# A loop of 62 rounds over four 50 KB buffers in place of straight code, in a log-softmax

## Chip, cores and metric

The kernel runs on one core of a Trainium2 chip. The metric is device time in microseconds (us), median over the executions of a kernel; lower is better. All executions quoted here were fast (granted TensorE clock 1.00). A ratio is the mean time of one kernel's fast runs over that of the kernel before in the same rounds on the same chip, with a 95% interval; it is not quite the ratio of the medians that stand beside it.

## The reference

`x` is float32 of shape (16, 512, 50000): 8192 rows, 1638.4 MB in and as much out.

```python
max_x = np.max(x, axis=-1, keepdims=True)
shifted = x - max_x
log_sum_exp = np.log(np.sum(np.exp(shifted), axis=-1, keepdims=True))
return (shifted - log_sum_exp).astype(np.float32)
```

## The kernel before

A row lies on G = 8 partitions, so that a tile is 16 rows: 128 partitions of 6250 columns (25,000 bytes), 512 tiles. There are 8 buffers. SyncE issues the loads, ScalarE's queue issues the stores, and each store writes from the buffer that its load filled. The program is straight code: the Python loop emits every tile with constant addresses.

```python
G = 8; R = P // G; EXP_C = 3125; NBUF = 8; AHEAD = 7
    xt = xf.rearrange("(t r) (g w) -> t (r g) w", r=R, g=G)
    ot = of.rearrange("(t r) (g w) -> t (r g) w", r=R, g=G)
    data = ctx.enter_context(tc.tile_pool(name="data", bufs=NBUF))
# ... (other pools, the matrix of ones)
    def load(t):
        buf = data.tile([P, W], FP32, name="buf")
        nc.sync.dma_start(out=buf, in_=xt[t])
        tiles[t] = buf
    def front(t):
        buf = tiles[t]
        pmax = stats.tile([P, 1], FP32, name="pmax")
        nc.vector.reduce_max(out=pmax, in_=buf, axis=AX)
        # ... two transposes, a reduction and a copy: negmax, the row's own maximum
        for j in range(nexp):                                   # 2 pieces
            nc.scalar.activation(
                out=dump, in_=buf[:, j * EXP_C : (j + 1) * EXP_C], func=ACT.Exp,
                bias=negmax[:, 0:1], scale=1.0, accum_out=part[:, j : j + 1],
            )
        # ... 2 matmuls with ones: rowsum;  Ln: logsum
    def back(t):
        buf = tiles.pop(t)
        nc.vector.tensor_scalar(
            out=buf, in0=buf, scalar1=shift.pop(t)[:, 0:1], scalar2=logs.pop(t),
            op0=ALU.add, op1=ALU.subtract,
        )
        nc.scalar.dma_start(out=ot[t], in_=buf)

    for t in range(AHEAD):
        load(t)
    for t in range(ntiles + 1):
        if t < ntiles: front(t)
        if t >= 1: back(t - 1)
        if t + AHEAD < ntiles: load(t + AHEAD)
```

Of the kernel before, what the change touches and what calls it, by code (L numbers as in the profile page):

```python
# [1 line left out]

# [4 lines left out]


FP32 = mybir.dt.float32
ACT = mybir.ActivationFunctionType  # L10
ALU = mybir.AluOpType
AX = mybir.AxisListType.X

P = 128
SQ = 32

G = 8
R = P // G
EXP_C = 3125
NBUF = 8  # L20
AHEAD = 7


@with_exitstack
def kernel(
    ctx: ExitStack,
    tc: tile.TileContext,
    x: bass.AP,
    out: bass.AP,
):  # L30
    nc = tc.nc
    xf = x.flatten_outer_dims()
    of = out.flatten_outer_dims()
    N, V = xf.shape
    W = V // G
    assert N % R == 0 and V % G == 0 and W % EXP_C == 0
    ntiles = N // R
    nexp = W // EXP_C

    xt = xf.rearrange("(t r) (g w) -> t (r g) w", r=R, g=G)  # L40
    ot = of.rearrange("(t r) (g w) -> t (r g) w", r=R, g=G)

    data = ctx.enter_context(tc.tile_pool(name="data", bufs=NBUF))
    stats = ctx.enter_context(tc.tile_pool(name="stats", bufs=4))
    consts = ctx.enter_context(tc.tile_pool(name="consts", bufs=1))
    dump_pool = ctx.enter_context(
        tc.tile_pool(name="dump", bufs=1, space=bass.MemoryType.PSUM)
    )
    sum_pool = ctx.enter_context(
        tc.tile_pool(name="sums", bufs=1, space=bass.MemoryType.PSUM)  # L50
    )

    ctx.enter_context(tc.manual_schedule())


    ones = consts.tile([P, P], FP32)
    nc.gpsimd.memset(ones, 1.0)  # L57
    ones3 = ones.rearrange("p (r g) -> p r g", g=G)
    nc.gpsimd.affine_select(  # L59
        out=ones3, in_=ones3, pattern=[[-G, R], [0, G]], base=0,  # L60
        channel_multiplier=1, compare_op=ALU.is_ge, fill=0.0,
    )
    nc.gpsimd.affine_select(  # L63
        out=ones3, in_=ones3, pattern=[[G, R], [0, G]], base=G - 1,
        channel_multiplier=-1, compare_op=ALU.is_ge, fill=0.0,
    )
    nc.scalar.preload_act_table_set("natural_log_exp_and_others")  # L67

    tiles = {}
    shift = {}  # L70
    logs = {}

    def load(t):
        buf = data.tile([P, W], FP32, name="buf")
        nc.sync.dma_start(out=buf, in_=xt[t])
        tiles[t] = buf

    def front(t):
        buf = tiles[t]
        pmax = stats.tile([P, 1], FP32, name="pmax")  # L80
        nc.vector.reduce_max(out=pmax, in_=buf, axis=AX)  # L81

        allmax = stats.tile([P, SQ], FP32, name="allmax")
        nc.vector.transpose(out=allmax, in_=pmax.to_broadcast([P, SQ]))  # L84
        rowmax = stats.tile([P, SQ // G], FP32, name="rowmax")
        nc.vector.tensor_reduce(  # L86
            out=rowmax, in_=allmax.rearrange("p (r g) -> p r g", g=G),
            op=ALU.max, axis=AX, negate=True,
        )
        spread = stats.tile([P, SQ], FP32, name="spread")  # L90
        nc.vector.tensor_copy(  # L91
            out=spread.rearrange("p (r g) -> p r g", g=G),
            in_=rowmax[:, :, None].to_broadcast([P, SQ // G, G]),
        )
        negmax = stats.tile([P, SQ], FP32, name="negmax")
        nc.vector.transpose(out=negmax, in_=spread)  # L96
        shift[t] = negmax

        part = stats.tile([P, nexp], FP32, name="part")
        for j in range(nexp):  # L100
            dump = dump_pool.tile([P, EXP_C], FP32, name="dump")
            nc.scalar.activation(  # L102
                out=dump, in_=buf[:, j * EXP_C : (j + 1) * EXP_C], func=ACT.Exp,
                bias=negmax[:, 0:1], scale=1.0, accum_out=part[:, j : j + 1],
            )
        rowsum = sum_pool.tile([P, 1], FP32, name="rowsum")
        for j in range(nexp):
            nc.tensor.matmul(  # L108
                rowsum, ones, part[:, j : j + 1], start=j == 0, stop=j == nexp - 1
            )  # L110
        logsum = stats.tile([P, 1], FP32, name="logsum")
        nc.scalar.activation(out=logsum, in_=rowsum, func=ACT.Ln)  # L112
        logs[t] = logsum

    def back(t):
        buf = tiles.pop(t)
        nc.vector.tensor_scalar(  # L117
            out=buf, in0=buf, scalar1=shift.pop(t)[:, 0:1], scalar2=logs.pop(t),
            op0=ALU.add, op1=ALU.subtract,
        )  # L120
        nc.scalar.dma_start(out=ot[t], in_=buf)

    for t in range(AHEAD):
        load(t)
    for t in range(ntiles + 1):
        if t < ntiles:
            front(t)
        if t >= 1:
            back(t - 1)
        if t + AHEAD < ntiles:  # L130
            load(t + AHEAD)


# [1 line left out]
_INS = ['x']  # L135
_OUTS = [((16, 512, 50000), 'float32')]


# [23 lines left out]
```

## Time and profile before

| | before |
|---|---|
| time, median of 5 runs | 7614.19 us (7613.97 to 7615.95) |
| span in the profile | 7612.6 us |
| bytes moved, mean rate | 3277 MB, 431 GB/s |
| one tile of 16 rows | 14.8 us |

The page cuts the span in 40 slices; the row named DMA gives the busy share of the 16 DMA engines in tenths, the row named GB/s what they moved. A packet of data is one contiguous piece of one partition (25,000 or 50,000 bytes here), moved by one of the 16 DMA engines. A transfer lands when the semaphore that counts its finished packets is full; what waits for it starts then. The lines themselves are in the prediction.

### The profile page before, as it was taken

How to read it: one execution, taken by the hardware profiler on the slowest of the kernel's cores; microseconds unless marked ns; L12 is line 12 of the kernel's file. 1: busy time of each engine (PE TensorE's matmuls, PEld its weight loads, DVE VectorE, ACT ScalarE, POOL GpSimd, SP SyncE). 2: the span in 40 equal slices, each digit the busy share in tenths (PEclk: the TensorE clock that was granted, in tenths of full speed). 3: DMA queues.
4: the chain of work that ended last, by engine and by line, in shares of the span. 5: the costliest groups of instructions: out<-in, count | busy, mean ns of one | idle time of the engine just before them, and what ended most of it. 6: DMA issues, size and time to landing. Idle time of an engine off the chain costs nothing.

```text
span 7612.6 us, 12833 instructions
## 1 busy us (share of the span) xinstructions
PE 600.6 (8%) x2048; PEld 513.2 (7%) x2048; DVE 5567.2 (73%) x3072; ACT 3153.1 (41%) x2561; POOL 1.2 (0%) x7
## 2 busy tenths in 40 slices
PE   0000000000000000000000000000000000000000
PEld 0000000000000000000000000000000000000000
DVE  7777777777777777777777777777777777777776
ACT  4444444444444444444444444444444444444443
POOL 0000000000000000000000000000000000000000
DMA  9999999999999999999999999999999999999998
GB/s 425 433 432 432 432 432 432 432 432 432 432 432 432 432 432 432 432 432 432 432 432 432 432 432 432 432 432 432 432 432 432 432 432 432 431 432 432 432 432 380
DMA packets 147540, 3277.68 MB, mean 431 GB/s; under 512 B 16384, under 2 KB 16384, under 8 KB 16384
## 3 DMA queue, kind: packets, MB, share of 16 engines
q1 hardware_dynamic: 73728, 1638.43, 50.0%
q10 hardware_dynamic: 73728, 1638.43, 50.0%
q14 instruction: 68, 0.56, 0.0%
q8 instruction: 16, 0.26, 0.0%
HBM read 1638.40 MB, written 1638.40 MB: 430 GB/s over the span
## 4 chain that ended last, share of the span: by engine, by line
DVE 73%; another core or an unknown queue 25%; issue 1%; DMA 0%; ACT 0%; PE 0%; ACTq 0%
DVE pmax L81 45%; DVE buf L117 23%; DVE allmax L84 1%; DVE rowmax L86 1%; DVE spread L91 1%; DVE negmax L96 0%; DMA buf<-in_x_dram 0%; ACT dump L102 0%; PE rowsum L108 0%; ACT logsum L112 0%; ACTq L102 0%
## 5 line engine op out<-in xcount | busy, mean ns | idle before, releaser
L81 DVE TENSOR_REDUCE pmax<-buf 128x1 f32<-128x6250 f32 x512 | 3411.8, 6664 | 1953.7 <-DMA buf<-in_x_dram 1953.7
L102 ACT ACTIVATE dump<-buf,negmax 128x3125 f32<-128x3125 f32 x1024 | 2938.1, 2869 | 4092.9 <-DVE negmax L96 4029.5
L117 DVE TENSOR_SCALAR buf<-buf,negmax,logsum 128x6250 f32<-128x6250 f32 x512 | 1789.7, 3496 | 4.5 <-ACT logsum L112 3.6
L108 PE MATMUL rowsum<-part,ones 128*128 128x1 f32 x2048 | 600.6, 363 | 6991.7 <-ACT dump L102 6991.7
L108 PEld LDWEIGHTS rowsum<-part,ones 128*128 128x128 f32 x2048 | 513.2, 311 | 7079.0 <-ACT dump L102 7057.2
L112 ACT ACTIVATE logsum<-rowsum 128x1 f32<-128x1 f32 x512 | 87.6, 171 | 345.8 <-PE rowsum L108 345.8
L102 ACT ACTIVATION_READ_ACCUMULATOR dump<-buf,negmax 128x1 f32 x1024 | 191.1, 187 | 0.0
L96 DVE STREAM_TRANSPOSE negmax<-spread 128x32 f32<-128x32 f32 x512 | 108.2, 211 | 17.7
L84 DVE STREAM_TRANSPOSE allmax<-pmax 128x32 f32<-128x32 f32 x512 | 108.3, 211 | 17.4
L86 DVE TENSOR_REDUCE rowmax<-allmax 128x4 f32<-128x32 f32 x512 | 95.3, 186 | 17.7
L91 DVE COPY spread<-rowmax 128x32 f32<-128x32 f32 x512 | 92.9, 181 | 17.8
L67 ACT ACT_TABLE_LOAD x1 | 1.3, 1283 | 0.8 <-PEq L146 0.8
L59 POOL TENSOR_SCALAR_AFFINE_SELECT ones<-ones 128x128 f32<-128x128 f32 x1 | 0.4, 403 | 0.1
L63 POOL TENSOR_SCALAR_AFFINE_SELECT ones<-ones 128x128 f32<-128x128 f32 x1 | 0.4, 397 | 0.1
L57 POOL MEMSET ones<- 128x128 f32 x1 | 0.2, 204 | 0.3 <-POOLq L146 0.3
L146 POOL MEMSET const-bfloat16-1.0<- 128x1 bf16 x1 | 0.1, 101 | 0.0
L146 POOL MEMSET const-uint8-127<- 128x1 uint8 x1 | 0.1, 101 | 0.0
L146 POOL MEMSET const-float32-0.0<- 128x1 f32 x1 | 0.1, 98 | 0.3 <-issue 0.3
L146 POOL MEMSET const-float32-1.0<- 128x1 f32 x1 | 0.1, 98 | 0.0
## 6 DMA issues: line engine op xcount, KB each, us to landing
buf<-in_x_dram SPq DMA_DIRECT2D x512, 3125.0 KB, 51.9
out_dram<-buf ACTq DMA_DIRECT2D x512, 3125.0 KB, 37.5
```

The costliest lines, as they stand in the source:

```text
L59: nc.gpsimd.affine_select(out=ones3, in_=ones3, pattern=[[-G, R], [0, G]], base=0, channel_multiplier=1, compare_op=ALU.is_ge, fill=0.0,)
L63: nc.gpsimd.affine_select(out=ones3, in_=ones3, pattern=[[G, R], [0, G]], base=G - 1, channel_multiplier=-1, compare_op=ALU.is_ge, fill=0.0,)
L67: nc.scalar.preload_act_table_set("natural_log_exp_and_others")
L81: nc.vector.reduce_max(out=pmax, in_=buf, axis=AX)
L84: nc.vector.transpose(out=allmax, in_=pmax.to_broadcast([P, SQ]))
L86: nc.vector.tensor_reduce(out=rowmax, in_=allmax.rearrange("p (r g) -> p r g", g=G), op=ALU.max, axis=AX, negate=True,)
L91: nc.vector.tensor_copy(out=spread.rearrange("p (r g) -> p r g", g=G), in_=rowmax[:, :, None].to_broadcast([P, SQ // G, G]),)
L96: nc.vector.transpose(out=negmax, in_=spread)
L102: nc.scalar.activation(out=dump, in_=buf[:, j * EXP_C : (j + 1) * EXP_C], func=ACT.Exp, bias=negmax[:, 0:1], scale=1.0, accum_out=part[:, ...
L108: nc.tensor.matmul(rowsum, ones, part[:, j : j + 1], start=j == 0, stop=j == nexp - 1)
L112: nc.scalar.activation(out=logsum, in_=rowsum, func=ACT.Ln)
L117: nc.vector.tensor_scalar(out=buf, in0=buf, scalar1=shift.pop(t)[:, 0:1], scalar2=logs.pop(t), op0=ALU.add, op1=ALU.subtract,)
```

## The change

The intent is a short program: one body of four tiles, run 62 times, in place of the code of 512 tiles. A row now lies on 4 partitions, a tile is 32 rows (12500 columns, 50,000 bytes on a partition), and there are 256 tiles in four fixed buffers. Each of four pieces of a tile is shifted by its own maximum, so that its Exp can start early; the sums are rescaled afterwards. Before the loop stands one round, and one after it. In the loop the address of a load and of a store comes from a register (`bass.ds(t, 1)`).

```diff
-G = 8
+G = 4
-NBUF = 8
-AHEAD = 7
+NBUF = 4
+    bufs = [data.tile([P, W], FP32, name=f"buf{j}") for j in range(NBUF)]
+    def dram(a, t):
+        return a[bass.ds(t, 1)].rearrange("o p w -> (o p) w")
+    def load(j, t):
+        nc.sync.dma_start(out=bufs[j], in_=dram(xt, t))
+    def compute(j, t):
+        for c in range(nexp):                                   # 4 pieces
+            piece = buf[:, c * EXP_C : (c + 1) * EXP_C]
+            nc.vector.tensor_reduce(
+                out=negm[:, c : c + 1], in_=piece, op=ALU.max, axis=AX, negate=True
+            )
+            nc.scalar.activation(
+                out=dump, in_=piece, func=ACT.Exp,
+                bias=negm[:, c : c + 1], scale=1.0, accum_out=part[:, c : c + 1],
+            )
 # ... (cut) negp and negmax as before; then
+        nc.scalar.activation(
+            out=scale, in_=negm, func=ACT.Exp, bias=negmax[:, 0:1], scale=-1.0
+        )
+        nc.vector.tensor_mul(out=scaled, in0=scale, in1=part)
 # ... (cut) 4 matmuls, Ln, the subtraction as before; then
-        nc.scalar.dma_start(out=ot[t], in_=buf)
+        nc.scalar.dma_start(out=dram(ot, t), in_=buf)
-    for t in range(AHEAD):
-        load(t)
-    for t in range(ntiles + 1):
-        if t < ntiles:
-            front(t)
-        if t >= 1:
-            back(t - 1)
-        if t + AHEAD < ntiles:
-            load(t + AHEAD)
+    def round_of(t, last=False):
+        for j in range(NBUF):
+            compute(j, t + j)
+            if not last:
+                load(j, t + j + NBUF)
+    for j in range(NBUF):
+        load(j, j)
+    round_of(0)
+    with tc.For_i(NBUF, ntiles - NBUF, NBUF, iteration_sync="reg_based") as t:
+        with tc.manual_schedule():
+            round_of(t)
+    round_of(ntiles - NBUF, last=True)
```

More of the change, by code (lines that the diff above doesn't have):

```diff
@@ L41 @@
     ot = of.rearrange("(t r) (g w) -> t (r g) w", r=R, g=G)
-    data = ctx.enter_context(tc.tile_pool(name="data", bufs=NBUF))
-    stats = ctx.enter_context(tc.tile_pool(name="stats", bufs=4))
+    data = ctx.enter_context(tc.tile_pool(name="data", bufs=1))
+    stats = ctx.enter_context(tc.tile_pool(name="stats", bufs=1))
     consts = ctx.enter_context(tc.tile_pool(name="consts", bufs=1))
@@ L67 @@
     nc.scalar.preload_act_table_set("natural_log_exp_and_others")
-    tiles = {}
-    shift = {}
-    logs = {}
-    def load(t):
-        buf = data.tile([P, W], FP32, name="buf")
-        nc.sync.dma_start(out=buf, in_=xt[t])
-        tiles[t] = buf
-    def front(t):
-        buf = tiles[t]
-        pmax = stats.tile([P, 1], FP32, name="pmax")
-        nc.vector.reduce_max(out=pmax, in_=buf, axis=AX)
-        allmax = stats.tile([P, SQ], FP32, name="allmax")
-        nc.vector.transpose(out=allmax, in_=pmax.to_broadcast([P, SQ]))
-        rowmax = stats.tile([P, SQ // G], FP32, name="rowmax")
+    bufs = [data.tile([P, W], FP32, name=f"buf{j}") for j in range(NBUF)]
@@ new lines, with pair @@
+    dump = dump_pool.tile([P, EXP_C], FP32, name="dump")
+    rowsum = sum_pool.tile([P, 1], FP32, name="rowsum")
+    def pair(shape, name):
+        return [stats.tile(shape, FP32, name=f"{name}{k}") for k in range(2)]
+    negms, parts, scales, scaleds = (
+        pair([P, nexp], n) for n in ("negm", "part", "scale", "scaled")
+    )
+    negps, logsums = pair([P, 1], "negp"), pair([P, 1], "logsum")
+    allnegs, spreads, negmaxs = (
+        pair([P, SQ], n) for n in ("allneg", "spread", "negmax")
+    )
@@ new lines @@
+    rownegs = pair([P, SQ // G], "rowneg")
+    def dram(a, t):
[3 more added lines that the diff above has]
+    def compute(j, t):
+        buf, k = bufs[j], j % 2
+        negm, part, scale, scaled = negms[k], parts[k], scales[k], scaleds[k]
+        negp, logsum = negps[k], logsums[k]
+        allneg, spread, negmax, rowneg = allnegs[k], spreads[k], negmaxs[k], rownegs[k]
+        for c in range(nexp):
[6 more added lines that the diff above has]
+                bias=negm[:, c : c + 1], scale=1.0, accum_out=part[:, c : c + 1],
+            )
+        nc.vector.tensor_reduce(out=negp, in_=negm, op=ALU.min, axis=AX)
+        nc.vector.transpose(out=allneg, in_=negp.to_broadcast([P, SQ]))
@@ L86, in front @@
         nc.vector.tensor_reduce(
-            out=rowmax, in_=allmax.rearrange("p (r g) -> p r g", g=G),
-            op=ALU.max, axis=AX, negate=True,
+            out=rowneg, in_=allneg.rearrange("p (r g) -> p r g", g=G),
+            op=ALU.min, axis=AX,
         )
-        spread = stats.tile([P, SQ], FP32, name="spread")
         nc.vector.tensor_copy(
             out=spread.rearrange("p (r g) -> p r g", g=G),
-            in_=rowmax[:, :, None].to_broadcast([P, SQ // G, G]),
+            in_=rowneg[:, :, None].to_broadcast([P, SQ // G, G]),
@@ L94, in front @@
         )
-        negmax = stats.tile([P, SQ], FP32, name="negmax")
         nc.vector.transpose(out=negmax, in_=spread)
-        shift[t] = negmax
-        part = stats.tile([P, nexp], FP32, name="part")
-        for j in range(nexp):
-            dump = dump_pool.tile([P, EXP_C], FP32, name="dump")
-            nc.scalar.activation(
-                out=dump, in_=buf[:, j * EXP_C : (j + 1) * EXP_C], func=ACT.Exp,
-                bias=negmax[:, 0:1], scale=1.0, accum_out=part[:, j : j + 1],
-            )
@@ L106, in front @@
-        rowsum = sum_pool.tile([P, 1], FP32, name="rowsum")
-        for j in range(nexp):
-            nc.tensor.matmul(
-                rowsum, ones, part[:, j : j + 1], start=j == 0, stop=j == nexp - 1
-            )
-        logsum = stats.tile([P, 1], FP32, name="logsum")
+        nc.scalar.activation(
+            out=scale, in_=negm, func=ACT.Exp, bias=negmax[:, 0:1], scale=-1.0
+        )
+        nc.vector.tensor_mul(out=scaled, in0=scale, in1=part)
+        for c in range(nexp):
+            nc.tensor.matmul(
+                rowsum, ones, scaled[:, c : c + 1], start=c == 0, stop=c == nexp - 1
+            )
@@ L112, in front @@
         nc.scalar.activation(out=logsum, in_=rowsum, func=ACT.Ln)
-        logs[t] = logsum
-    def back(t):
-        buf = tiles.pop(t)
         nc.vector.tensor_scalar(
-            out=buf, in0=buf, scalar1=shift.pop(t)[:, 0:1], scalar2=logs.pop(t),
+            out=buf, in0=buf, scalar1=negmax[:, 0:1], scalar2=logsum,
             op0=ALU.add, op1=ALU.subtract,
         )
-        nc.scalar.dma_start(out=ot[t], in_=buf)
-    for t in range(AHEAD):
-        load(t)
-    for t in range(ntiles + 1):
-        if t < ntiles:
-            front(t)
-        if t >= 1:
-            back(t - 1)
-        if t + AHEAD < ntiles:
-            load(t + AHEAD)
+        nc.scalar.dma_start(out=dram(ot, t), in_=buf)
@@ L135 @@
+    def round_of(t, last=False):
[3 more added lines that the diff above has]
+                load(j, t + j + NBUF)
+    assert ntiles % NBUF == 0 and ntiles >= 3 * NBUF
+    for j in range(NBUF):
[5 more added lines that the diff above has]
+    round_of(ntiles - NBUF, last=True)
 _INS = ['x']
```

## The prediction

> **What bounds the kernel now.** I read the page first: the slices, the queues, then the groups.
>
> ```profile
> span 7612.6 us, 12833 instructions
> ...
> DMA  9999999999999999999999999999999999999998
> GB/s 425 433 432 432 432 432 432 432 432 432 432 432 432 432 432 432 432 432 432 432 432 432 432 432 432 432 432 432 432 432 432 432 432 432 431 432 432 432 432 380
> ...
> q1 hardware_dynamic: 73728, 1638.43, 50.0%
> q10 hardware_dynamic: 73728, 1638.43, 50.0%
> ...
> DVE 73%; another core or an unknown queue 25%; issue 1%; DMA 0%; ACT 0%; PE 0%; ACTq 0%
> ...
> L81 DVE TENSOR_REDUCE pmax<-buf 128x1 f32<-128x6250 f32 x512 | 3411.8, 6664 | 1953.7 <-DMA buf<-in_x_dram 1953.7
> L102 ACT ACTIVATE dump<-buf,negmax 128x3125 f32<-128x3125 f32 x1024 | 2938.1, 2869 | 4092.9 <-DVE negmax L96 4029.5
> L117 DVE TENSOR_SCALAR buf<-buf,negmax,logsum 128x6250 f32<-128x6250 f32 x512 | 1789.7, 3496 | 4.5 <-ACT logsum L112 3.6
> ...
> buf<-in_x_dram SPq DMA_DIRECT2D x512, 3125.0 KB, 51.9
> out_dram<-buf ACTq DMA_DIRECT2D x512, 3125.0 KB, 37.5
> ```
>
> The 16 DMA engines are busy in every slice and move 432 GB/s; the load queue (q1) and the store queue (q10) each take half of them. The chain of waits names VectorE, but its 25% of "unknown queue" is VectorE waiting for loads: 1953.7 us of idle time before the maximum. So the DMA engines are the bound. A load takes 51.9 us from issue to landing and a store 37.5 us, though a period is 7585/512 = 14.8 us: some 3.5 loads and 2.5 stores are queued at any time, so no engine ever runs dry. What releases a load is in the waits of the load queue:
>
> ```profile
> SPq L75 <- DMA out_dram<-buf: 7305.6, 504, 26.8
> ```
>
> Each load waits for the store that frees its buffer. From the page's bytes: 3276.8 MB at 432 GB/s is 7585 us; the other 27 us are some 2 us of start and a tail in which the engines thin out, as the windows near the end show (the last two columns are DMA share and GB/s):
>
> ```profile
> 7570.00:7580.00 10.00, 1.18 (x4) 1.01 (x4) 6.07 (x6) 6.16 (x5) 0.00 (x0) 1.00 0.42 180
> ```
>
> **What the Trainium skill says.** "DMA: Bandwidth & Descriptors", Specifications, gives a fabric ceiling of 435 GB/s; the trace's 432 is 99% of it, so a large gain is not to be had. The same page, "Queues, rings and completion order", says that each engine goes round its queue rows, a packet at a time; the two equal halves of the queue lines agree, and so do the trace's packet times in the first 100 us, where loads and stores alternate. Its "Anatomy of one DMA" puts a fixed cost of about 2.0 us on a DMA, mostly the receipt at the end. Here the first load is issued at 0.8 us and VectorE starts at 11.05 us; 3.2 MB at 432 GB/s are 7.4 us, so a lone load carries 2.8 us. "VectorE: DVE Perf Modes", "Mode 2×_2P", says that an fp32 operation with one SBUF source can make two results a cycle: the row of L117 (3496 ns for 6250 columns, against 6664 for the maximum of L81) agrees. The doubled width keeps this.
>
> **The change, part by part.**
>
> *Bytes and packets.* The bytes are the same. A tile is 6.4 MB each way, 256 tiles, and a period at 432 GB/s is 12.8 MB / 432 = 29.63 us. A packet is a row of a partition, so it grows from 25,000 to 50,000 bytes: 25,000 bytes take 0.926 us of one engine (16 engines at 432 GB/s), a packet of 50,000 then 1.85 us. Half as many packets may save up to 0.4% (the distance from 432 to 435 at most is 0.7%). I count 0.
>
> *Engines per tile.* VectorE: four maxima of 3125 columns at half of 6664 ns plus some fixed time, 3.42 us each, 13.7 us; the last Exp then runs 3.0 us on (2869 ns and the accumulator's 187, overlapped a little), the small chain of transposes hides under it; scale, product, four matmuls (before, one took 0.6 us: 2.4), Ln and their waits 3.5 us; the subtraction 2 x 3496 less its fixed part, 6.8 us. Sum 27.0 us. VectorE, ScalarE and TensorE are now in series within a tile, where before the work of two tiles was interleaved. 27.0 is under 29.63, so it stays hidden, with 2.6 us to spare instead of 3.8 us in 14.8.
>
> *The loop.* The built program shows no barrier on the back edge: engines count on in registers. It shows two new waits. (1) Inside the loop every store waits for the store before it: addresses are registers now, and writes to the output count as overlapping. So one store is in flight instead of 2.5, and one or two loads. ScalarE's queue is held by this wait; the next tile's Exps start only after the store's issue: 4 x 3.02 (but not before the last maximum), then 3.5 and 6.8, about 25 us after the issue, again under 29.63. (2) On leaving the loop SyncE waits for every DMA of the loop, loads of the last four tiles included, before a barrier.
>
> *Cost of (2), on the path.* The last load in the loop goes out when the store of tile 251 has landed: 14.8 + 2.8 = 17.6 us. Barrier 1.5 (estimate). Then four tiles of compute with nothing before them, 4 x 27.0 = 108, and the last store, 14.8 + 1.5 = 16.3. Together 143 us, in which the DMA engines have five transfers, 5 x 14.8 = 74: a loss of 69 us, in place of the old tail's 25.
>
> *Cost of (1), on the path or not.* When a store lands, the next store and one load are issued at the same moment. The gap of the store queue, from the last byte to the next store's first byte, I put at 1.45 us: 0.4 from the last packet to the landing of its semaphores, 0.05 from landing to the issue (both from the trace's records), and 0.85 to 1.0 from issue to first packet (the store issued at 7592.47 us moves its first bytes in the window from 7593.0). Queues alternate, and if the store goes first, each engine still holds one load packet when the store's last packet is done: 1.85 us of work. 1.45 is less than 1.85, so the gap is covered and the period stays 29.63 us.
>
> *Sum.* Start 2 + 256 x 29.63 = 7585 + exit 69 = 7656 us; I predict 7660, 0.6% slower.
>
> **The rivals.**
>
> A. *The gap is not covered.* If the load reaches the engines before the store, the store's packet is the last of the 16, no load is left at its end, and both queues are empty for the gap: the period is 29.63 + 1.6 = 31.2 us in 248 tiles, 400 us more, about 8050 us (+6%). For it: both are released by one event and issued at almost the same moment, so the order is a race of a tenth of a microsecond, and the first store under a backlog of loads took over 3 us from issue to first packet, so an engine takes in packets ahead. Against it: a store's first packet follows its issue sooner (0.85 us against 1.0 to 1.8 for the first loads). If the order changes from tile to tile, or the gap with register addresses is 2.2 us, the result lies between, 7700 to 7900.
>
> B. *The engines become the bound.* The chain of 27.0 us would have to pass 29.63. If waits on registers and the hold on ScalarE made it 31, the time would be near 8000. I see no single term that is 3 us off.
>
> C. *A gain.* The old trace has engines that lag behind the others at the end (a few carry packets alone from 7570 to 7577 us); short code fetches fewer instructions, and larger packets could bring 432 towards 435. That is at most 0.7%, 50 us, and the exit takes 69 back: about 7610.
>
> **Range and chances.** The covered case with C in part gives 7610 to 7690: 6 in 10. Between: 1 in 10. A in full, to 8050: nearly 3 in 10. The limit of 2% is 7766. So same 0.62, slower 0.36, faster 0.02; the range is 7600 to 8030.
>
> **What would show it.** Right: slices at 432 GB/s or above to the last but one; load and store each some 30 us from issue to landing; ScalarE's queue waiting for the store before the store's issue; in the last 130 us a DMA share near one half, with four tiles 27 us apart. A right instead: GB/s near 410 in all slices, and DMA share falling to zero for 1.5 us in each period of 31 us. B right: the maximum no longer waits for a load, and VectorE with its waits for ScalarE fills the period. Wrong altogether would be a wait that I have not seen in the loop, such as one that empties the DMA queues at each back edge.

## The result, and the profile after

The changed kernel takes 9880.04 us, median of 5 runs (9870.1 to 9891.83): ratio 1.298 (1.296 to 1.2995), 30% slower. Its results are correct. The prediction was 7660 with a range of 7600 to 8030, so the measured time is far outside it.

Lines of the page of the kernel after:

```profile
span 9878.1 us, 18331 instructions
...
DMA  9988988989899898998988989989898998988986
GB/s 389 343 331 329 335 328 333 334 327 333 328 335 332 327 335 326 335 333 326 332 331 331 336 325 334 333 330 336 328 335 329 336 333 327 334 328 332 334 330 274
...
q1 hardware_dynamic: 36864, 1638.42, 46.4%
q10 hardware_dynamic: 36864, 1638.42, 43.0%
...
L101 ACT ACTIVATE dump<-buf,negm 128x3125 f32<-128x3125 f32 x1024 | 2936.9, 2868 | 6131.3 <-DMA out_dram<-buf 4362.7
L98 DVE TENSOR_REDUCE negm<-buf 128x1 f32<-128x3125 f32 x1024 | 3416.3, 3398 | 142.2 <-PEq L173 74.7
...
buf<-in_x_dram SPq DMA_DIRECT2D x256, 6250.0 KB, 38.3
out_dram<-buf ACTq DMA_DIRECT2D x256, 6250.0 KB, 38.5
```

All slices but the first two and the last move 325 to 336 GB/s instead of 432, so the loss is in every period of the loop. The DMA row alone would mislead: it shows 8 or 9 tenths. Idle time explains only a part; the rest is in the q lines. They give packets, MB and share: 46.4% of 16 engines x 9878 us, over 36,864 packets, is 2.0 us a packet if all are counted; only 32,768 of them are rows of data, the others are tiny, so a load's packet takes 0.464 x 16 x 9878 / 32768 = 2.24 us and a store's 2.07 us. The same bytes in the same two queues took 1.85 us each at the old rate (the prediction's estimate, which the runs without the wait confirm below). And the last two lines: load and store both land some 38 us after their issue, one whole period: there is one of each in flight.

The waits of the load queue, after (total, times, longest):

```profile
SPq L88 <- DMA out_dram<-buf: 9571.9, 252, 81.0
```

A load still waits for the store that frees its buffer. The timeline of the kernel after shows what else that landing releases. Columns: start, duration, engine, line, operation; in brackets the idle time before it and its releaser. The row marked x2 merges two load issues, of which this is the first; the other comes with the store at 3060.57.

```profile
3021.35 39.53 SPq L88 DMA_DIRECT2D buf<-in_x_dram  x2
3021.37 0.36 ACTq L132 DMA_DIRECT2D out_dram<-buf  x1
3021.98 2.87 ACT L101 ACTIVATE dump<-buf,negm 128x3125 f32<-128x3125 f32 x1 [23.27 <-DMA out_dram<-buf]
...
3036.59 6.79 DVE L128 TENSOR_SCALAR buf<-buf,negmax,logsum 128x12500 f32<-128x12500 f32 x1 [2.16 <-ACT logsum L127]
...
3060.57 0.36 ACTq L132 DMA_DIRECT2D out_dram<-buf  x1
```

Load and store are issued 0.02 us apart, the load first. Both had been waiting for the same event, the landing of the store before: the load because it needs the buffer, the store because in the loop its address is a register, and two writes to the output with register addresses are kept in order (the built program has this wait). The next store's data is ready at 3036.59 + 6.79 = 3043.4, but it is issued only at 3060.57, 17 us later. So no compute engine sets this period, although the page shows ScalarE idle for 4362.7 us behind stores. ScalarE is idle because the store's wait stands ahead of its Exps in its queue.

The windows of 2 us at the seam between two periods (last columns: clock, DMA share, GB/s). Packets are counted where they start, so that a share can pass 1:

```profile
3018.00:3020.00 2.00, 0.00 (x0) 0.00 (x0) 1.74 (x6) 0.00 (x0) 0.00 (x0) 1.00 0.29 125
3020.00:3022.00 2.00, 0.00 (x0) 0.00 (x0) 0.00 (x0) 0.02 (x1) 0.00 (x0) 1.00 0.00 0
3022.00:3024.00 2.00, 0.00 (x0) 0.00 (x0) 0.00 (x0) 2.00 (x1) 0.00 (x0) 1.00 1.81 400
```

From 3020 to 3022 not one packet of data starts on any of the 16 engines (only the 4-byte packets that count a landing do); in the 2 us before, only few do. All engines run dry, and they start together. One window of 40 us, of the kernel after and then of the kernel before, gives the size:

```profile
3000.00:3040.00 40.00, 1.87 (x8) 1.78 (x8) 23.32 (x12) 12.32 (x10) 0.00 (x0) 1.00 0.91 338
```

```profile
3000.00:3040.00 40.00, 2.93 (x10) 2.51 (x10) 30.03 (x18) 13.98 (x14) 0.00 (x0) 1.00 1.00 432
```

**Where the 2265 us are.** From the loop's first maximum at 170.45 us to the landing of its last store at 9739.8 us lie 9569.4 us for 248 tiles, 38.59 us a tile. At the old rate, 7585 / 256 = 29.63 us, they would be 7348: 2221 of the 2265.5 us of difference in span are in the loop. The other 8 tiles take 308.7 us instead of 8 x 29.63 + 27 = 264: 45 us for entering and leaving the loop. Those show as two single waits of VectorE, which are longer than 45 us because transfers go on during a part of them:

```profile
DVE negm L98 <- PEq L173: 74.7, 1, 74.7
DVE negm L98 <- SPq L144: 48.7, 1, 48.7
```

**One period in packets.** The trace records every packet. It doesn't name the engine, but packets can be put on one by matching each end to the next start. In all 129 periods between 2000 and 7000 us the load's 8 packets and the store's 8 packets on an engine alternate, beginning with the load, so the store's last packet is the last of the 16. Then nothing is left in either queue until the landing has been counted and the next pair is issued. Measured between the subtractions of VectorE, which are one period apart, a period is 38.62 us; the packets of an engine add up to 34.65 us of it, and 3.97 us are idle. A load packet takes 2.250 us on average (the first of a period 3.5), a store packet 2.083, against a median of 1.847 where the queues never run dry (means of 1.848 to 1.861 in e1 and e2): 16 x 1.847 = 29.55. So the excess of 9.07 us is 5.1 us of longer packets and 4.0 us of idle time. The place in the round makes no difference (between store issues 38.55, 38.64, 38.61 and 38.61 us on average, with a scatter of 0.4 us each): no barrier at the back edge shows.

### The profile page after: what moved, and what is told of

It reads as the page before. It is cut to its first block, busy times and chain, and to the rows that moved or that the text cites. A ratio compares the mean times of both kernels' runs of the same rounds, so it can differ in the third digit from the quotient of the medians.

```text
span 9878.1 us, 18331 instructions
## 1 busy us (share of the span) xinstructions
PE 476.1 (5%) x2048; PEld 456.1 (5%) x2048; DVE 5417.1 (55%) x2816; ACT 3156.4 (32%) x2561; POOL 1.4 (0%) x7
## 3 DMA queue, kind: packets, MB, share of 16 engines
q1 hardware_dynamic: 36864, 1638.42, 46.4%
q10 hardware_dynamic: 36864, 1638.42, 43.0%
## 5 line engine op out<-in xcount | busy, mean ns | idle before, releaser
L101 ACT ACTIVATE dump<-buf,negm 128x3125 f32<-128x3125 f32 x1024 | 2936.9, 2868 | 6131.3 <-DMA out_dram<-buf 4362.7
L98 DVE TENSOR_REDUCE negm<-buf 128x1 f32<-128x3125 f32 x1024 | 3416.3, 3398 | 142.2 <-PEq L173 74.7
L128 DVE TENSOR_SCALAR buf<-buf,negmax,logsum 128x12500 f32<-128x12500 f32 x256 | 1738.2, 6790 | 561.5 <-ACT logsum L127 561.5
L124 PE MATMUL rowsum<-scaled,ones 128*128 128x1 f32 x2048 | 476.1, 354 | 9378.0 <-DVE scaled L122 9378.0
L124 PEld LDWEIGHTS rowsum<-scaled,ones 128*128 128x128 f32 x2048 | 456.1, 328 | 9397.9 <-DVE scaled L122 7024.8
L101 ACT ACTIVATION_READ_ACCUMULATOR dump<-buf,negm 128x1 f32 x1024 | 190.8, 186 | 0.0
L119 ACT ACTIVATE scale<-negm,negmax 128x4 f32<-128x4 f32 x256 | 72.1, 282 | 0.0
L116 DVE STREAM_TRANSPOSE negmax<-spread 128x32 f32<-128x32 f32 x256 | 54.1, 211 | 13.2
L107 DVE STREAM_TRANSPOSE allneg<-negp 128x32 f32<-128x32 f32 x256 | 54.2, 212 | 8.9
L108 DVE TENSOR_REDUCE rowneg<-allneg 128x8 f32<-128x32 f32 x256 | 47.5, 186 | 8.9
## 6 DMA issues: line engine op xcount, KB each, us to landing
buf<-in_x_dram SPq DMA_DIRECT2D x256, 6250.0 KB, 38.3
```

The source lines that it names most:

```text
L98: nc.vector.tensor_reduce(out=negm[:, c : c + 1], in_=piece, op=ALU.max, axis=AX, negate=True)
L101: nc.scalar.activation(out=dump, in_=piece, func=ACT.Exp, bias=negm[:, c : c + 1], scale=1.0, accum_out=part[:, c : c + 1],)
L107: nc.vector.transpose(out=allneg, in_=negp.to_broadcast([P, SQ]))
L108: nc.vector.tensor_reduce(out=rowneg, in_=allneg.rearrange("p (r g) -> p r g", g=G), op=ALU.min, axis=AX,)
L116: nc.vector.transpose(out=negmax, in_=spread)
L119: nc.scalar.activation(out=scale, in_=negm, func=ACT.Exp, bias=negmax[:, 0:1], scale=-1.0)
```

## The experiments

The theory after reading the result, **the wait**: the write-after-write wait of register-addressed stores leaves one store and one load in flight, both released by one landing, the load first, and the engines run dry once a period. Its rivals: **the loop** itself (registers, back edge, barriers) is slow; **the tile** is (50 KB buffers, the order of compute); or **the hold**: the wait holds ScalarE's Exps, and the compute chain becomes the bound.

All runs, with the kernels before and after as ends of the scale. Period, busy and idle are per tile and engine, from the packet records between 2000 and 7000 us as above, idle being period less busy (where the queues never run dry it comes out at -0.03 to -0.05, which shows the accuracy). Tiles of 25 KB are half as large, so that their periods are to be doubled for a comparison.

| run | time us (runs) | ratio (95%) | period | busy | idle | load, store packet |
|---|---|---|---|---|---|---|
| before, 25 KB | 7614.19 (5) | 1 | 14.86 | 14.89 | -0.04 | 0.928, 0.928 |
| after, 50 KB | 9880.04 (5) | 1.298 (1.296-1.2995) | 38.62 | 34.65 | 3.97 | 2.250, 2.083 |
| e1_views | 7690.53 (4) | 1.0107 (1.0088-1.0125) | 29.70 | 29.75 | -0.05 | 1.861, 1.848 |
| e2_straight | 7616.56 (4) | 1.0018 (0.9991-1.0044) | 29.73 | 29.76 | -0.03 | 1.860, 1.848 |
| e3_before_wait, 25 KB | 9379.99 (4) | 1.2323 (1.2302-1.2343) | 18.37 | 16.19 | 2.18 | 1.075, 0.949 |
| e4_one_queue | 8807.77 (2) | 1.1568 (1.1545-1.1591) | 34.16 | 31.52 | 2.64 | 1.971 both |
| e5_store_first | 7661.56 (2) | 1.0062 (1.0042-1.0083) | 29.72 | 29.76 | -0.04 | 1.858 both |
| e6_two_queues_store_first | 8101.04 (4) | 1.064 (1.0622-1.0657) | 31.50 | 30.70 | 0.80 | 1.927, 1.911 |
| e7_loop_8, 25 KB | 9454.97 (2) | 1.2418 (1.2393-1.2443) | 18.41 | 16.20 | 2.21 | 1.075, 0.950 |
| e8_straight_8, 25 KB | 7678.63 (4) | 1.0085 (1.0068-1.0102) | 14.95 | 14.98 | -0.03 | 0.936, 0.935 |
| e9_straight_wait | 9797.78 (2) | 1.2868 (1.2843-1.2894) | 38.26 | 34.57 | 3.69 | 2.244, 2.075 |
| e10_straight_wait_halves | 8825.42 (2) | 1.1591 (1.1568-1.1615) | 34.51 | 31.48 | 3.03 | 0.995, 0.973 |
| e11_straight_one_queue | 7601.6 (4) | 0.9984 (0.9967-1.0001) | 29.65 | 29.69 | -0.03 | 1.851 both |
| e12_halves_store_first | 7878.18 (2) | 1.0347 (1.0317-1.0377) | 30.70 | 30.43 | 0.27 | 0.944, 0.958 |

All gave correct results.

### e1_views: the loop without the wait

The output is declared as four views that don't overlap, one for each place in the round, so that only a store and the one four tiles earlier stay in order.

```diff
+    views = [
+        v.flatten_outer_dims().rearrange("(t r) (g w) -> t (r g) w", r=R, g=G)
+        for v in bass_types.dram_disjoint_views(out, NBUF)
+    ]
-        nc.scalar.dma_start(out=dram(ot, t), in_=buf)
+        nc.scalar.dma_start(out=dram(views[j], t), in_=buf)
```

> The loop as it is, but the output is named through four views that are told apart, one for each buffer, so that a store in the loop no longer waits for the store before it; nothing else changes. If the store-after-store wait is the cause: two stores can be queued again, packets take 1.85 us, the period falls to 29.6 us, and the time is 256 x 29.55 = 7565 + start 2 + loss at the loop's entry some 15 + loss at its exit some 64 = 7650 us (7600 to 7720). If instead the geometry is the cause (packets of 50 KB, four buffers, engines in series within a tile), it stays near 9880 us.

Measured: 7690.53 us, where the theory of the wait had put it. Lines of its page:

```profile
GB/s 400 407 433 432 433 434 433 433 431 432 430 433 429 433 429 431 430 428 430 431 431 432 433 433 432 433 433 433 433 433 432 433 433 433 433 433 433 433 434 262
...
buf<-in_x_dram SPq DMA_DIRECT2D x256, 6250.0 KB, 41.6
out_dram<-buf ACTq DMA_DIRECT2D x256, 6250.0 KB, 48.8
```

The loop stays, and the rate is back at 432. Loads and stores again take longer than a period of 29.7 us to land, which means that they queue. The loop and the tile are out as causes.

### e2_straight: the new body without the loop

```diff
-        return a[bass.ds(t, 1)].rearrange("o p w -> (o p) w")
+        return a[t]
-    with tc.For_i(NBUF, ntiles - NBUF, NBUF, iteration_sync="reg_based") as t:
-        with tc.manual_schedule():
-            round_of(t)
+    for t in range(NBUF, ntiles - NBUF, NBUF):
+        round_of(t)
```

> The changed kernel with the 62 rounds written out as straight code: same 50 KB buffers, same pieces, fixed addresses, so no wait between stores and no drain at entry and exit. If the wait between stores is the cause: 7565 + 2 + a tail of some 28 = 7595 us (7570 to 7640), at or a little below the kernel before. If the geometry is the cause: near 9880 us.

Measured: 7616.56 us, no different from before. So 50 KB buffers, four maxima and one row on 4 partitions cost nothing. e1 less e2, 74 us, is what entering and leaving the loop costs when its periods are full.

### e3_before_wait and e9_straight_wait: the wait alone

The wait is put into straight code: in e3 into the kernel before, in e9 into e2.

```diff
+        store = nc.scalar.dma_start(out=ot[t], in_=buf)
+        if stores:
+            tc.add_manual_dep(store.ins, stores[-1].ins.name, ...)   # data, synchronised
+        stores.append(store)
```

> The kernel before, straight code and eight 25 KB buffers, with one thing added: each store waits for the store before it. If this wait alone, with a load released by the same landing, is the cause, the fixed part of the 9.1 us that the loop loses per tile comes back for each of 512 smaller tiles: 14.8 + 4 to 9 us, so 19 to 24 us a tile, 9600 to 12200 us. If the loop or the large packets have to be there too, or if the four more buffers keep loads queued over the gap: 7620 to 7900 us.

> Straight code with the 50 KB buffers (7617 us without the wait), and the wait of each store for the store before it added by hand; no loop. If the wait carries the whole loss, the period of 38.6 us comes back: 252 x 38.6 + 130 = 9850 us (9700 to 9950). If the loop's register waits or its dynamic addresses add to it, clearly less: under 9400 us.

e9 measured 9797.78 us, 0.8% under the changed kernel, with the same packets (2.244 and 2.075 us) and nearly the same idle time (3.69 us). One wait in straight code brings back nearly the whole loss, so the loop is not needed for it. e3 measured 9379.99 us, just below the range that was expected: the wait takes the old kernel too, but costs 18.37 - 14.86 = 3.5 us per small tile, 7.0 per 32 rows, not quite the 8.5 of e9 (38.26 - 29.73). From the timeline of e3:

```profile
3012.27 18.93 SPq L76 DMA_DIRECT2D buf<-in_x_dram  x2
3012.28 0.36 ACTq L122 DMA_DIRECT2D out_dram<-buf  x1
...
3030.59 0.34 ACTq L122 DMA_DIRECT2D out_dram<-buf  x1
```

Even with 8 buffers, load and store go out together, the load 0.01 us ahead, once in 18.3 us: more buffers don't help, since each further load waits for a further store, and the stores come one at a time.

### e4_one_queue and e5_store_first: who is issued first

In e4 the store moves to SyncE's queue, where the load stands ahead of it. In e5 the loads are also emitted one tile later, so that the store stands ahead of the load that the same landing releases. Both keep the loop and the wait, and both take the wait off ScalarE.

```diff
-        nc.scalar.dma_start(out=dram(ot, t), in_=buf)
+        nc.sync.dma_start(out=dram(ot, t), in_=buf)
# only e5:
-            if not last:
-                load(j, t + j + NBUF)
+            if j == 0 and not first:
+                load(NBUF - 1, t + NBUF - 1)
+            if j > 0 and not last:
+                load(j - 1, t + j - 1 + NBUF)
```

> The loop with its waits, but stores issued by SyncE instead of ScalarE. When a store lands, SyncE issues the next load first and the next store 0.35 us later; ScalarE is no longer held by the wait between stores. If holding ScalarE (and so the Exps of the next tile) is the cause, the time falls to some 7700 us. If one store at a time is the cause by way of the DMA queues, nothing is gained: 9700 to 10000 us.

> As the run before, but the next load is written after the next store, so that SyncE issues the store first and the load 0.35 us later, both when a store has landed. If the order of the two is what uncovers the gap (as the prediction's rival A says), each engine keeps a load packet at the end of a store, the gap is covered and the period is 29.6 to 31 us: 7650 to 8000 us. If the gap is uncovered in any order (engines that have drifted apart, slower packets), it stays above 9300 us.

The timelines of e4, then of e5:

```profile
3031.50 0.34 SPq L88 DMA_DIRECT2D buf<-in_x_dram  x1
3032.05 0.35 SPq L132 DMA_DIRECT2D out_dram<-buf  x1
...
3065.77 0.34 SPq L88 DMA_DIRECT2D buf<-in_x_dram  x1
```

```profile
3028.46 0.34 SPq L132 DMA_DIRECT2D out_dram<-buf  x1
3029.06 0.35 SPq L88 DMA_DIRECT2D buf<-in_x_dram  x1
...
3058.12 0.34 SPq L132 DMA_DIRECT2D out_dram<-buf  x1
```

The two differ in the order of two issues 0.6 us apart, and by 1146 us in time (8807.77 against 7661.56, where the theory of the order had put e5). In one queue a transfer is carried whole before the next: e4's loads land 19.2 us after their issue, its stores 33.3. In e4 the store comes last: when it lands, nothing is left, and the period of 34.16 us has 2.64 us of idle time. In e5 the store comes first: when it lands, each engine still has its 8 load packets, 14.8 us of work, in which the next pair is issued; no idle time is left, although the wait is still there. That the e5 stores land 29.5 us after their issue, one period, while its loads take 43.7 us, says the same. The hold would have e4 near the old time, because ScalarE is free there; e4 stays 16% slower, so the hold is not the cause. But e4 missed the number that the theory of the wait had, 9700 to 10000: I had taken the loss for the same in one queue as in two. There the engines don't alternate, and their packets grow by 0.12 us (1.971 against 1.85), not by 0.32.

### e6_two_queues_store_first: the prediction's covered case

Two queues as in the changed kernel, but the load waits for a tick that ScalarE writes behind the store's issue.

```diff
         nc.scalar.dma_start(out=dram(ot, t), in_=buf)
+        return nc.scalar.activation(out=ticks[k], in_=negmax[:, 0:1], func=ACT.Exp)
+    # load(j, t, tick): add_manual_dep(load, tick); emitted one tile later, as in e5
```

> The loop with its waits and its two queues, but the next load also waits for a 0.2 us operation of ScalarE that stands behind the next store, so that the load is issued some 0.6 us after the store instead of 0.02 us before it. If the order of the two decides whether one load packet is left to cover the gap, the period is 29.6 to 31 us and the time 7650 to 8000 us. If the gap in two queues is uncovered in either order (the run with one queue left a whole load behind the store, not one packet), or if loads and stores that alternate in step slow each other's packets, the period stays over 34 us: above 8700 us.

Measured: 8101.04 us, between what the theories had. From its timeline:

```profile
3024.74 0.34 ACTq L141 DMA_DIRECT2D out_dram<-buf  x1
...
3025.36 30.27 SPq L89 DMA_DIRECT2D buf<-in_x_dram  x2
```

With the load 0.62 us behind the store, the store's first packet follows its issue after 0.85 us (median) and the load's after 4.9. In the changed kernel it is the other way round: 0.95 us for the load and 4.2 us for the store. The order takes the mean period from 38.62 to 31.50 us. It stays 1.9 us above 29.6: 0.80 us idle, 1.1 us of longer packets. But this mean is that of two kinds of period, which for long stretches take turns. The store issues:

```profile
2991.43 0.34 ACTq L141 DMA_DIRECT2D out_dram<-buf  x1
...
3024.74 0.34 ACTq L141 DMA_DIRECT2D out_dram<-buf  x1
...
3054.51 0.34 ACTq L141 DMA_DIRECT2D out_dram<-buf  x1
...
3087.68 0.34 ACTq L141 DMA_DIRECT2D out_dram<-buf  x1
```

They are 33.3, 29.8 and 33.2 us apart. Of 159 periods between 2000 and 7000 us, 74 take 33.3 us on average: one load packet an engine is left behind the store, and 1.67 us are idle. 62 take 29.5 us: three are left, and 0.02 us are idle. The other 23 lie between (31.0 us; 2.3 left, 0.09 us idle). So one load packet does not cover the gap, and two to three do. The packet records show the reason: the 4-byte packet that counts the store's last landing starts 1.84 us after the store's last data, one load packet later. In e12 below, with half-size packets, it starts 0.92 us later, and in the kernel after, where no load packet is left, at once (0.00). The packet that counts takes its turn with the other queue, so the load packet that should cover the gap also lengthens it.

### e7_loop_8 and e8_straight_8: the size of the tiles

The changed kernel (e7) and e2 (e8) with 25 KB tiles in 8 buffers.

```diff
-G = 4
+G = 8
-NBUF = 4
+NBUF = 8
```

> The changed kernel, loop and waits, with eight 25 KB buffers and tiles of 16 rows instead of four 50 KB buffers and 32 rows. If the loss per tile of 9.1 us is a fixed gap, it is paid 512 times: 24 us a tile, 12200 us. If only the 4.1 us that the one-queue run lost per tile are fixed and the rest grows with the bytes (slower packets): 14.8 + 4.1 + 2.5 = 21.4 us a tile, 11000 us. If more buffers cover the gap: below 8000 us.

> The changed kernel's pieces and order of work, as straight code with eight 25 KB buffers: the algorithm alone, without the loop and without the larger packets. DMA-bound as before: 512 x 14.82 = 7588 + 2 + a tail of 15 to 25: 7605 to 7620 us, the same as before. A gain would show that the shorter chain at the end pays.

e7 took 9454.97 us, which none of the expectations had. The loss of a landing is not a fixed 9 us, which twice as many landings would have doubled: with the small tiles it is 18.41 - 14.95 = 3.5 us, as in e3. e8 took 7678.63 us, 0.85% above before and above what was expected; its small tiles move at the full rate, and I didn't look for the cause of the 0.6% by which its period is longer.

### e10_straight_wait_halves and e12_halves_store_first: the size of the packets

e10 is e9 with each load and store in two halves of 6250 columns; both halves wait for both halves of the store before, so that there is still one landing per 32 rows, but the packets have 25,000 bytes. e12 also has the store issued first, by the tick of e6.

```diff
+    halves = [slice(0, H), slice(H, W)]
+        for h in halves:
+            dma = nc.sync.dma_start(out=bufs[j][:, h], in_=dram(xt, t)[:, h])
+        both = [nc.scalar.dma_start(out=dram(ot, t)[:, h], in_=buf[:, h]) for h in halves]
+        # every half depends on both halves of the store before; e12: loads also on the tick
```

> As the run before, but every load and every store is issued as two halves of 6250 columns, both halves released by the same landings as the whole was: the same bytes for each release, in packets of 25,000 bytes instead of 50,000. With 25,000-byte packets the two runs with that wait kept packets near 0.93 us. If large packets that alternate in step are what slows them to 2.1 us and more, most of the 5.1 us of extra packet time per tile goes and the period is 33 to 35 us: 8450 to 8950 us. If it is the bytes moved in step after each release, whatever the packet, the period stays near 38.6 us: over 9600 us.

> The fourth corner of order and packet size: straight code, each store waits for the store before it, two halves in 25,000-byte packets, and the loads wait for a small ScalarE operation behind the next store's two issues, so the store goes first. With 50,000-byte packets and the store first the period was 31.5 us, with 25,000-byte packets and the load first 34.5. If packet size and order act one by one: some 30 us, 7650 to 7800 us. If what is left at 31.5 us does not come from the packets but from the late load: 31 to 32.5 us, 7950 to 8350 us.

With 25 KB packets the same wait costs 34.51 - 29.73 = 4.8 us in place of 8.5: the packets' sum falls from 34.57 to 31.48 us, the idle time from 3.69 to 3.03. e12 took 7878.18 us, between the two windows that were expected. Periods with the wait, in two queues (us for 32 rows, 29.7 without the wait):

| | 50 KB packets | 25 KB packets |
|---|---|---|
| load first | 38.6 (after), 38.3 (e9) | 34.5 (e10) |
| store first | 31.5 (e6) | 30.7 (e12) |

Order matters most, and packet size matters where the load is first. Both values with the store first are means of periods that differ, in e12 too (28.1 to 33.9 us between store issues). "First" means first at the engines, and an issue that is ahead by a few hundredths of a us does not decide it. From the timeline of e10:

```profile
3016.16 0.87 ACTq L150 DMA_DIRECT2D out_dram<-buf  x2
3016.20 0.82 SPq L103 DMA_DIRECT2D buf<-in_x_dram  x2
```

In 144 of 145 periods of e10 the store's first half is issued before the load's, by 0.035 us (median), and yet in 91% of them the first packet is the load's.

### e11_straight_one_queue: a version that beats both?

e2 with the stores on SyncE's queue and the loads emitted one tile later; no wait between stores.

> A candidate: straight code, 50 KB buffers, no wait between stores, loads and stores both from SyncE with the next store ahead of the next load. Packets of 50,000 bytes give 29.55 us a tile, 7565 us, no loss at entry and exit of a loop, and a tail of 25 to 40: 7590 to 7610 us, at most 0.3% under the kernel before. If the single queue lets the engines drift as in the store-first loop (slices of 429 GB/s towards its end): 7620 to 7660 us.

Measured: 7601.6 us, ratio 0.9984 (0.9967 to 1.0001). It has the lowest time of all, as expected, but the interval touches 1: the same as before. There was nothing to gain, since the DMA engines are busy throughout.

## Why the prediction was wrong

Right were these steps:

- The DMA engines bound the kernel before. e2 and e11, with another body and other queues, stay within 0.2% of its time.
- The store waits for the store before it, and the page of the loop showed it. e1 and e9 show this wait to be the cause: without it 7691 us, with it alone 9798 us.
- No barrier at the back edge: the four places in the round differ by 0.09 us at most.
- The chain of a tile was put at 27.0 us; in the last round, where nothing else runs, the stores are issued 25.7 us apart. The exit was put at 143 us from the landing of the loop's last store; it took 9878.1 - 9739.8 = 138 us.
- Rival B is out: the store's data was ready 17 us before its issue, and e4 frees ScalarE without curing the loss. Rival C gained nothing that can be told from zero (e11).

**The step that failed** is in "Cost of (1)": "Queues alternate, and if the store goes first, each engine still holds one load packet when the store's last packet is done: 1.85 us of work. 1.45 is less than 1.85, so the gap is covered and the period stays 29.63 us." The store doesn't go first. The load is issued 0.028 us ahead of it (median), and is first at the engines in all 129 periods looked at. That is rival A, to which I gave nearly 3 in 10. I had decided against it by "a store's first packet follows its issue sooner (0.85 us against 1.0 to 1.8 for the first loads)". e6 shows that these 0.85 us belong to whoever comes first, not to stores. The prediction called the order "a race of a tenth of a microsecond"; here it came out the same way every time. The 0.028 us are not the reason: in e10 the store's issue is 0.035 us ahead, and the load still moves first in nine periods of ten.

**The size of rival A failed too**: 31.2 us was predicted for its period, 38.6 was measured, which is why even the range fell short (its top, 8030, lay under rival A's own 8050). Two terms:

- The gap: 1.6 us predicted, 3.97 measured as mean idle time of an engine. The engines don't end together. The last store packet of all ends 0.65 us before the next issue, but the engine that is done first has by then been idle for 4.0 us, and 0.92 us pass from the issue to the first packet. Counted from the last byte, 0.65 + 0.92 = 1.57 us is just what I had predicted; but that is the shortest of 16 gaps.
- The packets: unchanged in the prediction, 2.25 and 2.08 us in the runs instead of 1.85. That is 5.1 us a period, more than the gap. No term of the sum stood for it.

**The covered case itself was too low**: with the store first the mean period is 31.50 us (e6), not 29.63, so that even that outcome would have been 8101 us, outside the range. The sum "1.45 is less than 1.85" fails: while a load packet is left, the packet that counts the landing comes 1.84 us after the last data, the issue 0.48 us after it, and the first packet 0.85 us after the issue. These 3.2 us are more than one load packet of 1.85 us; two to three of them (e6), or a whole transfer in the same queue (e5), cover them.

**A wait was missed**: on entering the loop VectorE waits 48.7 us once, because the loop starts only when all stores of the first round have landed. It is small beside the rest: entry and exit together make 45 us.

What stays open: why packets grow when the queues start again together after each gap. The longer first load packet of a period (3.5 us) is 1.65 of the 5.1 us. In the runs without the wait loads and stores share the engines as well, and their packets keep to 1.85 us; there the engines have drifted apart (in the kernel before 8.0 loads are in flight on average with a scatter of 2.5, in the kernel after 7.5 with a scatter of 5.7). That starting in step is the cause was not tested by itself. Many loads at one time are not enough for it: in e2 the 1353 load packets with 14 or more loads in flight on average took 1.849 us. Nor is it known what puts the load first at the engines when both are issued within 0.04 us, nor why the packets of e6 are still 1.1 us longer in sum.

## What to carry to other kernels

When code goes into a loop, look in the built program for what register addresses put in order: here it was store after store, and declaring the output as views that don't overlap took 9880 us back to 7691. When one landing releases several transfers, ask what is still in the DMA queues at that moment and which of the released ones comes first at the engines: a store ahead of the load in one queue hid the same wait (7662 us). In two queues, count in that the landing itself is late by a packet of the other queue (1.84 us in e6). And measure a gap as the mean over the 16 engines, with the packets' own durations beside it; here the longer packets cost more than the gap.

## What the Trainium skill lacked or had wrong

- "DMA: Bandwidth & Descriptors", "Queues, rings and completion order": that an engine goes round its queues packet by packet agrees with the alternating packets here. It doesn't say that a packet's duration depends on how the queues run: 50,000-byte packets took 1.85 us in queues that never ran dry, 2.25 (loads) and 2.08 (stores) where all queues emptied once a period; 25,000-byte packets 0.93, then 1.07 and 0.95.
- The same page, "Issuing engines are not separate DMA queues", says that issuing from several engines only saves the sequencer's time. Without a wait this agrees (7617 us with two queues, e2, and 7602 with one, e11). With one store in flight it doesn't hold: load first took 9880 us in two queues and 8808 in one, store first 8101 in two and 7662 in one (the pairs differ besides in that e4 and e5 free ScalarE of the wait and e6 has the tick).
- No page that I read says that stores with register addresses in a loop may be ordered one behind the other, or what one landing that releases both a load and a store costs: 3.5 us with 25 KB tiles, 8.5 to 8.9 us with 50 KB tiles.
- No page that I read gives a figure for how long a landing is held up by the other queue: 1.84 us with 50,000-byte packets (e6), 0.92 us with 25,000-byte packets (e12), 0.00 us where the other queue is empty (the kernel after).
